# The up-projection of a convolutional FFN: seven quarter products in place of eight, gated activations kept in DRAM

## The chip, the cores and the metric

One core of a Trainium2 chip. The program is launched once and runs from start to end without loops at run time. The metric is the device time of one run in microseconds (us); before, three runs were taken, and their median counts.

## The reference, cut to what matters

Float32, 1024 tokens of 1024 features. Two layers (gated spatial mixing and attention side by side), one layer of gated linear attention (GLA), then the FFN that the change is about, then a last norm:

```python
def conv_ffn(x, w_up, conv_w, conv_b, w_down):
    s = x.shape[1]
    u = x @ w_up                                   # [1024, 1024] @ [1024, 5632]
    u_pad = jnp.pad(u, ((0, 0), (CONV_WIDTH - 1, 0), (0, 0)))
    u = sum(u_pad[:, j:j + s] * conv_w[j] for j in range(CONV_WIDTH)) + conv_b
    gate, up = jnp.split(u, 2, axis=-1)            # 2816 columns each
    return (jax.nn.silu(gate) * up) @ w_down       # [1024, 2816] @ [2816, 1024]
```

The input of `conv_ffn` is `rms_norm(x, norm2)`, and its output is added to `x`.

## The kernel before, in words

**Products.** A float32 product runs as three matmuls over an exact split `x = hi + lo` (`hi` is `x` rounded to float32r): hi·hi, hi·lo and lo·hi (`steps3`, L158). `split` (L71) makes the pair from a float32 tile: a cast for `hi`, on VectorE (DVE) at L75 or on ScalarE (ACT) at L73, and a subtraction for `lo` on DVE through `tt` (L57). Every matmul is issued at L63, in `mm`. TensorE is PE, its weight loads PEld; GpSimd is POOL.

**Order.** PE's instructions run in the order in which they are written (a manual schedule). For the other engines and for the DMA queues (nearly all transfers are issued by SyncE, SP) a scheduler sets the order at build time, from its own simulated times, the written order being the priority; each engine then runs its list strictly in that order, and waits are semaphores on tiles. Tiles come from pools by tag, each tag with a number of buffers (`bufs`); a new tile of a tag waits until the last readers of the buffer's former tile are done.

**Activations.** The normed activations are held transposed, features on the partitions: two slots `X0` and `X1` of 32 KiB per partition (`big`, L105), one for each half of the tokens, each with hi and lo, 8 feature tiles and 512 tokens. In other stages the same slots hold the attention's probabilities (`XB`, L438, and `XA`, L562), in the FFN's second half the split gated tiles and the sums (`gX`, L937, `acc`, L946). `to_T` (L142) transposes four tiles of 128x128 on PE into PSUM and splits them into the slot.

**Weights.** `Weights` (L112) streams packed chunks of 128x1024 float32 (512 KB) through buffers `raw` (2) and splits them into pairs `w` (3).

**Start.** 20 float32 products of the identity with itself (`N_WARM`, L249) keep PE busy while the first token tile and its weights arrive.

**Output projection of the GLA** (L863 to L883): eight token tiles; beside each, on PE, the transposes of a former tile's normed result (`turn_x`, L854), which fill `hT`, the FFN's input. The last tile's norm is made in tile `gpost` (L884) and is transposed within the FFN (L929). At the end of the last tile, `W.fill(3)` (L882) fetches the first three chunks of `w_up`.

**Up-projection** (L924 to L940). `w_up` is packed so that chunk 2i is a block of 128 gate columns and chunk 2i + 1 the block of 128 up columns that belongs to it, each with all 8 feature tiles; 44 chunks, 22 pairs. For each chunk and each half of the tokens `up_mm` (L903) issues 24 matmuls of 128x512 into a PSUM tile `u` of 128x1024. The first three chunks run over the first half of the tokens, then the transposes of the last token tile, then over the second half. `up_use` (L906) works on a finished `u`: ACT starts the convolution (`c = u * cw2 + cb`), DVE adds two shifted products (L911, L912); after the up block of a pair ACT makes a tanh and DVE two gate steps, the last into `gs` (L917), a tile that keeps all 22 gated blocks in SBUF (88 KB per partition).

**Down-projection** (L969 to L1000). For each half of the output columns, for each two of the 22 gated blocks: a chunk of `w_down` is split, `gsplit` (L919) splits two blocks of `gs` into two of four slots (cast and subtraction on DVE), and PE issues 48 matmuls into eight PSUM banks, one for each token tile. At the end the sums, the residual `acc` and the last norm.

Of the kernel before, what the change touches and what calls it, by code (L numbers as in the profile page):

```python
# [8 lines left out]
F32 = mybir.dt.float32  # L9
# [9 lines left out]
NT = 8  # L19
KT = 8  # L20
FT = 22
N_WARM = 20
# [14 lines left out]
def build(tc, a):  # L37
    """The whole forward pass on one core.

    Float32 products run as three float32r passes over an exact split x = hi + lo  # L40
    (hi = x rounded to float32r, lo = x - hi): hi*hi + hi*lo + lo*hi.
    """
# [62 lines left out]
    def big(i, dt=F32R):  # L105
        """One of the two 32 KiB slots that hold h^T, the attention's P^T and P, the last gate and sums."""
        return T(xpool, [128, 8192], f"X{i}", dt)

    def hT_half(i):
        return big(i).rearrange("p (s k t) -> p s k t", s=2, k=KT)  # L110
# [31 lines left out]
    def to_T(src, dst, c0, ps_pool, n, k0=0, tag="tr"):  # L142
        """dst[:, hi/lo, k0 + k, c0:c0 + 128] = src[:, 128 k:128 (k + 1)]^T, k < n."""
# [7 lines left out]
    def norm_scale(xt, xn, g, junk=None):  # L151
        """xn = rmsnorm(xt) * g"""
# [27 lines left out]
    class Norms:  # L180
        """The token tiles of one norm, two ahead of their transposes into h^T."""
# [19 lines left out]
        def turn(self, j, tag="tr"):  # L201
# [3 lines left out]
            to_T(self.ready[t][:, 512 * j:], self.hT[t // 4], (t % 4) * 128, self.ps, 4, 4 * j, tag)  # L205
# [11 lines left out]
    # ------------------------------------------------------------------ the first two layers  # L217
# [3 lines left out]
    W = Weights(["w_in0", "w_out0", "w_in1", "w_out1", "gla_w_in", "gla_w_out", "w_up", "w_down"],  # L221
# [4 lines left out]
    for l in range(2):  # L226
# [11 lines left out]
        # A: norm, projections, gated spatial mixing  # L238
# [6 lines left out]
        if l == 0:  # L245
# [100 lines left out]
        def rope(dst, sq, qn, ps, n, i, t):  # L346
            """dst = rope(rmsnorm(ps) * g) of n heads of 64 for token tile t; sq and qn are for its use."""
# [27 lines left out]
        def turn_k(t):  # L375
            """K^T of the two heads, each in both halves of the partitions."""
# [34 lines left out]
        def gate_b(u, ps, th):  # L411
            """silu(g_b)^T * 2, a block of 128 features by 512 tokens; 4 steps."""
            hf, j = 1 - u // 4, u % 4
            for k in range(0, KT, 2):
                steps3(ps, wcols(ws[j:j + 1], 128), lambda k, s: hT[hf][:, s, k, :], range(k, k + 2), 0, KT - 1)
# [15 lines left out]
        # B: attention and, one token tile behind, the output projection  # L431
# [6 lines left out]
        XB = big(1, F32).rearrange("p (u k) -> p u k", u=8)  # L438
        qf, ya = XB[:, 7, 0:512], XB[:, 7, 512:1024]
# [13 lines left out]
        def scores(g):  # L453
            """Group g = (token tile, kv head): S, its maximum, exp; 8 steps."""
# [3 lines left out]
            for hh in (0, 2, 1, 3):  # L458
# [9 lines left out]
                P[hh] = XB[:, count[1] % 7]  # L468
# [10 lines left out]
        def turn(g, u):  # L479
            """P^T of two heads for two key tiles, split; the gate over the row sums first."""  # L480
# [10 lines left out]
            PT = XA[:, count[0] % 8]  # L491
# [41 lines left out]
        def project(qt):  # L533
            """x_new(t) = x(t) + rmsnorm(y(t) w_out) * g_post; 16 steps."""
# [27 lines left out]
        XA = big(0).rearrange("p (u s k h t) -> p u s k h t", u=8, s=2, k=2, h=2)  # L562
# [4 lines left out]
        def step(*ks):  # L567
            """The next step of the oldest projection, if it is one of these, once for each unit (g, u)."""
# [7 lines left out]
        for g in range(2 * NT):  # L576
# [6 lines left out]
            for u in range(8):  # L583
# [33 lines left out]
    # ------------------------------------------------------------------ gated linear attention  # L617
# [27 lines left out]
    def f3(ps, L, R, start=True, stop=True):  # L645
        """ps (+)= L^T R of hi/lo pairs."""
# [65 lines left out]
    def chunks(h, v, rs, kT, sT, qq, gd):  # L712
        """The chunks of head h and their gated norm; two steps each."""
# [30 lines left out]
    for h in range(4):  # L744
# [4 lines left out]
        def of(x):  # L749
            """The hi and lo parts of tile t of a pair."""  # L750
# [20 lines left out]
        # k and q: feature-major, with their decays  # L771
# [313 lines left out]
```

## Time and profile before

| | |
|---|---|
| runs | 2269.79 us median of 3 (2268.68 to 2269.9) |
| profiled execution, first to last instruction (span) | 2268.4 us |
| the median of the runs over the profiled span | 1.4 us |
| up-projection in that execution | 1541.2 to 2020.9 us |
| down-projection and end | 2020.9 to 2268.4 us |

The profiled execution is known by its span alone: the clock of a run also takes in what lies around the first and the last instruction. In the rows below times are us from the span's start, unless marked ns; "x" is a number of instructions; `<-` in a name reads "written from", and after a bracket or bar it names what ended the wait. A matmul's own duration (389 ns) is longer than its share of a full queue, since matmuls overlap.

### The profile page before, as it was taken

The page shows a single profiled execution, that of the slowest core. Times are in us where ns is not written, and L with a number is a line of the kernel's source. Part 1 is how long each engine was busy: PE and PEld are TensorE (multiplying, and loading weights), DVE is VectorE, ACT ScalarE, POOL GpSimd, SP SyncE. Part 2 cuts the span into 40 slices and gives each one's busy share as a digit, 9 for nine tenths or more (in the row PEclk, how much of TensorE's full clock was granted, in tenths as well). Part 3 has the DMA queues.
Part 4 walks back from the last instruction along what each step waited for, and adds up shares of the span by engine and source line. Part 5 has one row for each costly group of instructions (what it writes and reads, how often), then busy time and mean ns, then how long its engine had stood idle before and what let it go on. Part 6 is the DMA issues. An engine that isn't in the chain of part 4 may idle for free.

```text
span 2268.4 us, 30078 instructions
## 1 busy us (share of the span) xinstructions
PE 2239.4 (99%) x12196; PEld 1923.9 (85%) x12196; DVE 1420.0 (63%) x2169; ACT 747.8 (33%) x1401; POOL 157.3 (7%) x210
## 2 busy tenths in 40 slices
PE   9999999999999999999999999999999999999998
PEld 7888888888788878888899999888888888888887
DVE  7545788888844578888755655645554555554644
ACT  4203276665212146666532322221111111111102
POOL 1004200000101500000100100100000000000000
PEclk9999999999999999999999999999999999999999
DMA  5131401114321231111411112532111111131111
GB/s 191 62 122 38 158 24 58 56 37 145 114 72 65 75 126 43 43 56 63 154 45 59 47 56 78 175 102 76 54 49 47 47 47 56 47 121 47 47 56 75
DMA packets 65036, 171.93 MB, mean 76 GB/s; under 512 B 7680, under 2 KB 20352, under 8 KB 64896
## 3 DMA queue, kind: packets, MB, share of 16 engines
q1 hardware_dynamic: 63888, 166.33, 22.0%
q10 hardware_dynamic: 1008, 3.67, 0.6%
q8 instruction: 96, 1.57, 0.3%
q14 instruction: 44, 0.36, 0.1%
HBM read 136.94 MB, written 33.03 MB: 75 GB/s over the span
## 4 chain that ended last, share of the span: by engine, by line
PE 92%; DVE 3%; ACT 2%; issue 1%; DMA 1%; POOL 0%; POOLq 0%; SPq 0%; ACTq 0%; DVEq 0%
PE mm L63 33%; PE u L63 21%; PE d L63 10%; PE po L63 7%; PE o L63 7%; PE S L63 6%; PE tr L490 4%; PE tr L147 1%; DVE X L57 1%; ACT X L66 1%; DVE nm L467 0%; POOL rs L57 0%; PE big L63 0%; ACT X L73 0%; PE tr L405 0%
## 5 line engine op out<-in xcount | busy, mean ns | idle before, releaser
L63 PE MATMUL mm<-w,X 128*128 128x512 f32 (+1 forms) x3072 | 552.2, 338 | 2.3 <-DVE w L57 1.3
L63 PEld LDWEIGHTS mm<-w,X 128*128 128x128 f32 x3072 | 476.7, 190 | 64.0 <-DVE w L57 2.1
L63 PE MATMUL u<-X,w 128*128 128x512 f32 x2112 | 479.3, 389 | 0.8 <-DVE xt L57 0.8
L63 PEld LDWEIGHTS u<-X,w 128*128 128x128 f32 x2112 | 396.2, 188 | 83.4 <-DVE xt L57 1.2
L57 POOL TENSOR_TENSOR rs<-ve,nhalf 128x1 f32<-128x1 f32 (+2 forms) x136 | 109.8, 808 | 2078.6 <-DVE ve L93 2077.7
L63 PE MATMUL d<-w,X 128*128 128x512 f32 x1056 | 240.0, 389 | 0.2 <-DVE X L57 0.2
L57 DVE TENSOR_TENSOR X<-tr,X 128x512 fp32r<-128x512 f32 x300 | 204.4, 684 | 47.9 <-ACT X L73 44.9
L63 PEld LDWEIGHTS d<-w,X 128*128 128x128 f32 x1056 | 198.0, 188 | 41.9 <-DVE X L57 0.9
L75 DVE CAST w<-raw 128x1024 fp32r<-128x1024 f32 x132 | 93.2, 707 | 214.6 <-PE u L63 192.7
L73 ACT CAST X<-tr 128x512 fp32r<-128x512 f32 x300 | 173.5, 585 | 142.1 <-PE tr L490 77.4
L57 DVE TENSOR_TENSOR w<-raw,w 128x1024 fp32r<-128x1024 f32 x160 | 195.3, 1222 | 3.5 <-ACT w L73 1.0
L63 PE MATMUL S<-K,qT 128*128 128x512 f32 x512 | 178.9, 430 | 2.6 <-DVE t L60 1.4
L467 DVE TENSOR_REDUCE nm<-S 128x1 f32<-128x1024 f32 x128 | 155.9, 1218 | 25.6 <-PE S L63 25.2
L63 PEld LDWEIGHTS po<-X,V 128*128 128x128 f32 x1024 | 151.6, 189 | 22.8 <-DVE ol L57 6.8
L63 PE MATMUL po<-X,V 128*128 128x256 f32 x1024 | 167.7, 287 | 2.0 <-DVE ol L57 1.8
L66 ACT ACTIVATE X<-S,nm 128x1024 f32<-128x1024 f32 x128 | 142.9, 1116 | 62.2 <-DVE nm L467 62.0
L66 ACT ACTIVATE c<-u,cb,cw 128x1024 f32<-128x1024 f32 x44 | 53.2, 1208 | 317.5 <-PE u L63 317.5
L63 PE MATMUL mm<-X,w 128*128 128x512 f32 x672 | 155.5, 390 | 0.0
L490 PE MATMUL tr<-ident,X 128*128 128x128 f32 x960 | 144.7, 273 | 4.7 <-ACT qT L406 2.1
L63 PEld LDWEIGHTS mm<-X,w 128*128 128x128 f32 x672 | 125.3, 188 | 25.5
L490 PEld LDWEIGHTS tr<-ident,X 128*128 128x128 f32 x960 | 110.7, 139 | 12.4 <-DVE X L57 3.9
L60 DVE SCALAR_TENSOR_TENSOR c<-u,cw,c 128x1023 f32<-128x1023 f32 x88 | 112.6, 1280 | 1.5
(207 smaller groups left out, 2302.2 us busy)
## 6 DMA issues: line engine op xcount, KB each, us to landing
raw<-w_in SPq DMA_DIRECT2D x46, 512.0 KB, 3.5
raw<-w_up SPq DMA_DIRECT2D x44, 512.0 KB, 3.3
xt<-x SPq DMA_DIRECT2D x37, 512.0 KB, 3.7
raw<-gla_w_in SPq DMA_DIRECT2D x24, 512.0 KB, 3.6
raw<-w_down SPq DMA_DIRECT2D x22, 512.0 KB, 3.3
raw<-w_out SPq DMA_DIRECT2D x16, 512.0 KB, 3.3
x<-xt SPq DMA_DIRECT2D x16, 512.0 KB, 2.6
y<-yA SPq DMA_DIRECT2D x16, 256.0 KB, 2.0
```

What stands on the lines that cost most here:

```text
L57: (eng or nc.vector).tensor_tensor(out=out, in0=in0, in1=in1, op=op)
L60: nc.vector.scalar_tensor_tensor(out=out, in0=in0, scalar=scalar, in1=in1, op0=op0, op1=op1)
L63: nc.tensor.matmul(out, lhsT, rhs, start=start, stop=stop)
L66: nc.scalar.activation(out=out, in_=in_, func=func, **kw)
L73: nc.scalar.copy(hi, src)
L75: nc.vector.tensor_copy(hi, src)
L147: nc.tensor.transpose(ps[:, k], src[:, (j + k) * 128:(j + k + 1) * 128], ident)
L467: nc.vector.reduce_max(out=nm, in_=ps, axis=AX.X, negate=True)
L490: nc.tensor.transpose(ptr[:, k, e], P[pr + 2 * e][:, kt * 128:kt * 128 + 128], ident)
```

## The change

`w_up` and the activations are each taken as a 2x2 matrix of quarters: activations A11, A12 (first 512 tokens; first and last 512 features), A21, A22 (last 512 tokens), weights of a pair B11, B21 (up columns; first and last 512 features) and B12, B22 (gate columns). Eight products of quarters become seven, in Winograd's form of Strassen's algorithm: S1 = A21 + A22, S2 = S1 - A11, S3 = A11 - A21, S4 = A12 - S2; T1 = B12 - B11, T2 = B22 - T1, T3 = B22 - B12, T4 = B21 - T2; P1 = A11·B11, P2 = A12·B21, P3 = S4·B22, P4 = A22·T4, P5 = S1·T1, P6 = S2·T2, P7 = S3·T3. The results are up, first half: P1 + P2; gate, first half: P1 + P6 + P5 + P3; gate, second half: P1 + P6 + P7 + P5; up, second half: P1 + P6 + P7 + P4. P1, P6, P7 and P4 add up in one PSUM bank, which is read between them; P5 and P3 in another.

With it: the slots `X0`, `X1` become four quarter slots, here and in all earlier stages; S1 and S3 of the last four token tiles are formed while these are transposed; the sums of weights are made by POOL; `gs` goes to DRAM block by block, and `gsplit` loads it back and casts on ACT; `acc` gets a tile of its own; 10 warm-up products in place of 20, and seven wide ones.

The diff (comments, docstrings and what only follows the new slots are left out):

```diff
-N_WARM = 20
+N_WARM = 10
...
-    def big(i, dt=F32R):
-        return T(xpool, [128, 8192], f"X{i}", dt)
+    def quarter(i, dt=F32R):
+        return T(xpool, [128, 4096], f"X{i}", dt)
+    def hT_quarter(i):
+        return quarter(i).rearrange("p (s k t) -> p s k t", s=2, k=4)
     def hT_half(i):
+        return [hT_quarter(2 * i), hT_quarter(2 * i + 1)]
...
+            wide = [T(psL, [128, 512], "mm", bufs=6) for _ in range(2)]
+            for _ in range(3):
+                mm(wide[0], identr, identr.unsqueeze(1).broadcast_to([128, 4, 128]), True, True)
+            for _ in range(2):
+                for e in range(2):
+                    r = identr[64 * e:64 * e + 64]
+                    mm(wide[e], r, r.unsqueeze(1).broadcast_to([64, 4, 128]), True, True)
...
-    hT = [hT_half(0), hT_half(1)]
+    A11, A12, A22 = (hT_quarter(i) for i in range(3))
+    sums = quarter(3, F32).rearrange("p (s k t) -> p s k t", s=2, k=4)
+    S1f, S3f = sums[:, 0], sums[:, 1]
...
+    def quarters(t, xn, ps_pool):
+        if t < 4:
+            for j, A in enumerate((A11, A12)):
+                to_T(xn[:, 512 * j:], A, t * 128, ps_pool, 4)
+                yield
+            return
+        c = slice((t - 4) * 128, (t - 3) * 128)
+        p21 = four_T(xn, ps_pool)
+        tt(S3f[:, :, c], A11[:, 0, :, c], p21, ALU.subtract)
+        nc.scalar.copy(S1f[:, :, c], p21)
+        tt(S3f[:, :, c], S3f[:, :, c], A11[:, 1, :, c], ALU.add)
+        yield
+        p22 = four_T(xn[:, 512:], ps_pool)
+        split(A22[:, 0, :, c], A22[:, 1, :, c], p22, on_act=True)
+        tt(S1f[:, :, c], S1f[:, :, c], p22, ALU.add)
+        yield
...
+    def up_load(p):
+        raws[p] = [T(pF, [128, 1024], "rawx", bufs=2) if p % 2 else T(W.p, [128, 1024], "raw", bufs=2)
+                   for _ in range(2)]
+        for i in range(2):
+            load(raws[p][i], a["w_up"][2 * p + 1 - i])
+    def w_pair(i):
+        if i in (3, 5) or i > 5 and i % 4 == 1:
+            return T(pU, [128, 2, 1024], "wx", F32R)
+        return T(W.p, [128, 2, 1024], "w", F32R, bufs=3)
...
-                W.fill(3)
+                up_load(0)
+                ops[0] = [w_pair(0)]
+                split(ops[0][0][:, 0], ops[0][0][:, 1], raws[0][0], on_act=True)
...
-    gs = T(pF, [128, FT, 1024], "gs")
+    g_d = T(dram, [FT * 128, 1024], "gs")
...
+    def up_ops(p):
+        r1, r2 = raws.pop(p)
+        lo, hi = slice(0, 512), slice(512, 1024)
+        w = ops.setdefault(p, [])
+        if not w:
+            w.append(w_pair(3 * p))
+            split(w[0][:, 0], w[0][:, 1], r1, on_act=True)
+        t23 = T(pU, [128, 1024], "t23")
+        tt(t23[:, hi], r2[:, hi], r2[:, lo], ALU.subtract, nc.gpsimd)
+        tt(r2[:, lo], r2[:, lo], r1[:, lo], ALU.subtract, nc.gpsimd)
+        tt(t23[:, lo], r2[:, hi], r2[:, lo], ALU.subtract, nc.gpsimd)
+        tt(r1[:, hi], r1[:, hi], t23[:, lo], ALU.subtract, nc.gpsimd)
+        for src in (r2, t23):
+            w.append(w_pair(3 * p + len(w)))
+            split(w[-1][:, 0], w[-1][:, 1], src, on_act=True)
+        w.append(T(pU, [128, 2, 512], "w4", F32R, bufs=2))
+        split(w[3][:, 0], w[3][:, 1], r1[:, hi], on_act=True)
+    def product(ps, p, i, half, A, first, last=True):
+        w = ops[p][i]
+        c = 512 * half
+        for k in range(4):
+            L = [w[:, s, c + 128 * k:c + 128 * k + 128] for s in range(2)]
+            R = [A[:, s, k, :] for s in range(2)]
+            for n, (x, y) in enumerate(((0, 0), (0, 1), (1, 0))):
+                nc.tensor.matmul(ps, L[x], R[y], start=first and k == n == 0, stop=k == 3 and n == 2,
+                                 skip_group_check=True)
+    def bank(tag):
+        return T(psU, [128, 512], tag, bufs=3)
+    def P1(p):
+        s = st[p] = {"a": bank("a"), "up": T(pU, [128, 1024], "up", bufs=2)}
+        product(s["a"], p, 0, 0, A11, True)
+        nc.scalar.copy(s["up"][:, t1], s["a"])
+    def P2(p):
+        b = bank("b")
+        product(b, p, 0, 1, A12, True)
+        add(st[p]["up"][:, t1], b)
+    def P5(p):
+        s = st[p]
+        s["c"], s["gate"] = bank("b"), T(pU, [128, 1024], "gate", bufs=2)
+        product(s["c"], p, 1, 0, S1, True)
+        nc.scalar.copy(s["gate"][:, t2], s["c"])
+    def P6(p):
+        s = st[p]
+        product(s["a"], p, 2, 0, S2, False)
+        nc.scalar.copy(s["gate"][:, t1], s["a"])
+    def P3(p):
+        s = st[p]
+        product(s["c"], p, 1, 1, S4, False)
+        add(s["gate"][:, t1], s.pop("c"))
+    def P7(p):
+        s = st[p]
+        product(s["a"], p, 2, 1, S3, False)
+        add(s["gate"][:, t2], s["a"])
+    def P4(p):
+        s = st[p]
+        product(s["a"], p, 3, 0, A22, False)
+        nc.scalar.copy(s["up"][:, t2], s["a"])
     def gsplit(n):
-        gT = gX[:, n % 4]
-        split(gT[:, 0], gT[:, 1], gs[:, n % FT])
+        raw = T(pF, [128, 1024], "rawx", bufs=2)
+        load(raw, tok(g_d, n % FT))
+        gT = gX[n % 4]
+        split(gT[:, 0], gT[:, 1], raw, on_act=True)
         return gT
+    def conv(u, j, tag):
+        c = T(cst, [128, 1024], tag)
+        act(c, u, AF.Identity, scale=cw[:, j, 2:3], bias=cb[:, j:j + 1])
+        stt(c[:, 1:], u[:, :1023], cw[:, j, 1:2], c[:, 1:], ALU.mult, ALU.add)
+        stt(c[:, 2:], u[:, :1022], cw[:, j, 0:1], c[:, 2:], ALU.mult, ALU.add)
+        return c
+    def gated(p):
+        g = conv(st[p].pop("gate"), p, "gpre")
+        th = st[p]["th"] = T(pU, [128, 1024], "th")
+        act(th, g, AF.Tanh, scale=0.5)
+        stt(th, th, 1.0, g, ALU.add, ALU.mult)
+    def stored(p):
+        s = st.pop(p)
+        c = conv(s["up"], FT + p, "gpost")
+        stt(s["th"], s["th"], 0.5, c, ALU.mult, ALU.mult)
+        load(tok(g_d, p), s["th"])
+        del ops[p]
+    up_ops(0)
+    up_load(1)
+    P1(0)
+    P2(0)
+    up_ops(1)
+    for _ in quarters(NT - 1, xn, psU):
+        pass
+    P1(1)
+    P2(1)
+    for p in range(2):
+        b = bank("b")
+        product(b, p, 3, 0, A22, True)
+        nc.scalar.copy(st[p]["up"][:, t2], b)
...
+    for k in pairs:
+        split_sum(S1, k, S1f[:, k])
+    for s2, k in zip(tmp, pairs):
+        tt(s2, S1f[:, k], A11[:, 0, k], ALU.subtract)
+        tt(s2, s2, A11[:, 1, k], ALU.subtract)
+        split_sum(S2, k, s2)
+    for k in pairs:
+        split_sum(S3, k, S3f[:, k])
+    S4 = hT_quarter(3)
+    for s2, k in zip(tmp, pairs):
+        tt(s2, A12[:, 0, k], s2, ALU.subtract)
+        tt(s2, s2, A12[:, 1, k], ALU.add)
+        split_sum(S4, k, s2)
...
+    P5(0)
+    P5(1)
+    P6(0)
+    P7(0)
+    sum21(0)
+    P3(0)
+    gated(0)
+    stored(0)
+    up_load(2)
+    P6(1)
+    P7(1)
+    sum21(1)
+    up_ops(2)
+    P3(1)
+    gated(1)
+    stored(1)
+    for p in range(2, FT):
+        if p + 1 < FT:
+            up_load(p + 1)
+        P1(p)
+        P2(p)
+        P5(p)
+        if p > 2:
+            P4(p - 1)
+            stored(p - 1)
+        P6(p)
+        if p + 1 < FT:
+            up_ops(p + 1)
+        else:
+            W.fill(2, True)
+        P3(p)
+        P7(p)
+        gated(p)
...
+    gTs = [gsplit(k) for k in range(2)]
+    P4(FT - 1)
+    stored(FT - 1)
     sU.close()
...
-    acc = big(1, F32).rearrange("p (t c) -> p t c", t=NT)
+    acc = T(pD, [128, NT, 1024], "acc")
```

(`xn` is the normed tile; `split_sum` splits two of four feature tiles of a sum on ACT and DVE; `sum21` adds bank `a` to `up`'s second half; `pairs` are the two halves of the feature tiles, `tmp` two tiles of 128x1024.)

## Rows read from the trace of the kernel before

**Rows 1.** The page: span, and each engine's busy time, share and instructions.

```profile
span 2268.4 us, 30078 instructions
PE 2239.4 (99%) x12196; PEld 1923.9 (85%) x12196; DVE 1420.0 (63%) x2169; ACT 747.8 (33%) x1401; POOL 157.3 (7%) x210
```

**Rows 2.** Chain that ended last, 1500 to 2060 us: start, duration, what.

```profile
1541.19 11.19 PE u L63 x48
1552.37 0.87 PE tr L147 x8
1553.25 467.85 PE u L63 x2064
```

**Rows 3.** Windows: stretch, length, busy PE, PEld, DVE, ACT, POOL, clock, DMA share, GB/s.

```profile
1541.20:2020.90 479.70, 479.70 (x2120) 397.32 (x2121) 247.90 (x224) 77.40 (x69) 0.55 (x1) 1.00 0.15 50
```

**Rows 4.** Waits of PE, 1541 to 2030 us: in total, times, longest.

```profile
PE u L63 <- DVE xt L57: 0.8, 1, 0.8
```

**Rows 5.** Groups by shape, 1541 to 2021 us: busy us, mean ns, idle before.

```profile
L60 DVE SCALAR_TENSOR_TENSOR c<-u,cw,c 128x1022 f32<-128x1022 f32 x43 | 55.1, 1281 | 1.5
...
L57 DVE TENSOR_TENSOR w<-raw,w 128x1024 fp32r<-128x1024 f32 x43 | 52.7, 1226 | 1.4
L66 ACT ACTIVATE c<-u,cb,cw 128x1024 f32<-128x1024 f32 x43 | 52.0, 1208 | 312.2 <-PE u L63 312.2
L75 DVE CAST w<-raw 128x1024 fp32r<-128x1024 f32 x43 | 29.8, 694 | 192.7 <-PE u L63 192.7
L60 DVE SCALAR_TENSOR_TENSOR th<-th,c 128x1024 f32<-128x1024 f32 x22 | 27.0, 1225 | 23.7 <-ACT th L66 23.7
...
L66 ACT ACTIVATE th<-c 128x1024 f32<-128x1024 f32 x22 | 23.3, 1061 | 74.6 <-DVE c L60 74.6
```

**Rows 6.** Groups by shape, whole span: operations that the change issues more of.

```profile
L57 DVE TENSOR_TENSOR X<-tr,X 128x512 fp32r<-128x512 f32 x300 | 204.4, 684 | 47.9 <-ACT X L73 44.9
L73 ACT CAST X<-tr 128x512 fp32r<-128x512 f32 x300 | 173.5, 585 | 142.1 <-PE tr L490 77.4 <-PE tr L147 61.1
L73 ACT CAST w<-raw 128x1024 fp32r<-128x1024 f32 x28 | 29.5, 1053 | 178.7 <-PE d L63 174.2 <-DMA raw<-w_in 3.7 <-PE S L63 0.6
L57 DVE TENSOR_TENSOR xt<-xt,mm 128x512 f32<-128x512 f32 x16 | 11.0, 688 | 21.2 <-PE mm L63 19.9 <-DMA xt<-x 1.2
```

**Rows 7.** Line 57 on POOL: duration ns min/median/max, first and last start, shape.

```profile
L57 POOL TENSOR_TENSOR sq<-qn,tab x32: 730/1180/1582, 196.8 to 793.2; 128x256 f32<-128x256 f32 x32
...
L57 POOL TENSOR_TENSOR t<-t,tab x12: 313/325/375, 166.0 to 733.8; 128x64 f32<-128x64 f32 x12
```

**Rows 8.** Timeline of DVE and POOL, 196 to 204 and 231 to 247 us.

```profile
196.67 0.69 DVE L57 TENSOR_TENSOR t<-qn,tab 128x512 f32<-128x512 f32 x1
196.78 1.88 POOL L57 TENSOR_TENSOR sq<-qn,tab 128x256 f32<-128x256 f32 x2 [0.87 <-DVE qn L57]
...
234.28 2.73 POOL L57 TENSOR_TENSOR sq<-qn,tab 128x256 f32<-128x256 f32 x2 [0.87 <-DVE qn L57]
235.19 1.23 DVE L57 TENSOR_TENSOR t<-qn,tab 128x512 f32<-128x512 f32 x1
```

**Rows 9.** Timeline at the beginning of the up-projection: the last tile's norm.

```profile
1543.23 1.28 DVE L60 SCALAR_TENSOR_TENSOR gpost<-xt,rs,gpre 128x1024 f32<-128x1024 f32 x1 [0.73 <-POOL rs L57]
```

**Rows 10.** DMA issues: queue, how many, KB each, median us to landing.

```profile
raw<-w_up SPq DMA_DIRECT2D x44, 512.0 KB, 3.3
...
x<-xt SPq DMA_DIRECT2D x16, 512.0 KB, 2.6
```

**Rows 11.** Timeline of the start: warm-up, first norm, first weight cast, first transposes.

```profile
2.68 7.47 PE L63 MATMUL tr<-ident 128*128 128x128 f32 x40 [2.68 <-DMA ident<-cst]
...
7.04 1.28 DVE L60 SCALAR_TENSOR_TENSOR xn<-xt,rs,gpre 128x1024 f32<-128x1024 f32 x1 [0.67 <-POOL rs L57]
8.30 1.05 ACT L73 CAST w<-raw 128x1024 fp32r<-128x1024 f32 x1 [2.11 <-DMA raw<-w_in]
...
9.98 1.04 PE L147 MATMUL tr<-ident,xn 128*128 128x128 f32 x8
```

**Rows 12.** Windows at the start (columns as in rows 3).

```profile
6.00:9.00 3.00, 3.00 (x19) 3.00 (x18) 1.44 (x2) 0.89 (x3) 0.55 (x1) 1.00 1.02 411
```

More of the change, by code (lines that the diff above doesn't have):

```diff
@@ L414, in gate_b @@
             for k in range(0, KT, 2):
-                steps3(ps, wcols(ws[j:j + 1], 128), lambda k, s: hT[hf][:, s, k, :], range(k, k + 2), 0, KT - 1)
+                steps3(ps, wcols(ws[j:j + 1], 128), feat(hT[hf]), range(k, k + 2), 0, KT - 1)
                 if k < KT - 2:
@@ L437, in build @@
         g_pre = bcast(cst, a["pre_g"][1:2, :] if l == 0 else a["norm1"], 1024, "gpre")
-        XB = big(1, F32).rearrange("p (u k) -> p u k", u=8)
-        qf, ya = XB[:, 7, 0:512], XB[:, 7, 512:1024]
+        XB = [x[:, j] for x in (quarter(i, F32).rearrange("p (u k) -> p u k", u=4) for i in (2, 3)) for j in range(4)]
+        qf, ya = XB[7][:, 0:512], XB[7][:, 512:1024]
         count = [0, 0]
@@ L561, in build @@
             next(units[i // 4])
-        XA = big(0).rearrange("p (u s k h t) -> p u s k h t", u=8, s=2, k=2, h=2)
+        XA = [x[:, j] for x in (quarter(i).rearrange("p (u s k h t) -> p u s k h t", u=4, s=2, k=2, h=2)
+                                for i in (0, 1)) for j in range(4)]
         prep_load(0)
@@ L600, in build @@
                     i = NU.index(u) + 1
-                    norms.fetch(XB[:, i])
-                    norms.start(XB[:, i], XB[:, 3 if i < 3 else 4])
+                    norms.fetch(XB[i])
+                    norms.start(XB[i], XB[3 if i < 3 else 4])
         queue.append([project(NT - 1), 0])
@@ L677, in alpha_low @@
                 for s in range(2):
-                    mm(ps, was[:, k], hT[hf][:, s, k, :], k == 0 and s == 0, k == KT - 1 and s == 1)
+                    mm(ps, was[:, k], feat(hT[hf])(k, s), k == 0 and s == 0, k == KT - 1 and s == 1)
             sl = aT[:, hf * 512:hf * 512 + 512]
@@ L857, in turn_x @@
         norm_scale(xts.pop(t), xn, g_pre)
-        for j in (0, 4):
-            to_T(xn[:, 128 * j:], hT[t // 4], (t % 4) * 128, psH, 4, j)
-            yield
+        yield from quarters(t, xn, psH)
+    raws = {}
+    def up_load(p):
[7 more added lines that the diff above has]
+        return T(W.p, [128, 2, 1024], "w", F32R, bufs=3)
+    ops = {}
     xts, yrs = {}, {}
@@ L900, in build @@
     psU = opened_psum(sU, "psU")
[L901 to L917 removed]
+    S1, S2, S3 = (T(pU, [128, 2, 4, 512], f"S{i}", F32R) for i in range(1, 4))
@@ new lines, in product @@
+    def product(ps, p, i, half, A, first, last=True):
+        w = ops[p][i]
+        c = 512 * half
+        for k in range(4):
+            L = [w[:, s, c + 128 * k:c + 128 * k + 128] for s in range(2)]
[5 more added lines that the diff above has]
+        return T(psU, [128, 512], tag, bufs=3)
@@ new lines, in build, with add @@
+    st = {}
+    t1, t2 = slice(0, 512), slice(512, 1024)
+    def add(x, ps):
+        tt(x, x, ps, ALU.add)
+    def P1(p):
[11 more added lines that the diff above has]
+        nc.scalar.copy(s["gate"][:, t2], s["c"])
@@ L919, in gsplit @@
     def gsplit(n):
-        gT = gX[:, n % 4]
-        split(gT[:, 0], gT[:, 1], gs[:, n % FT])
-        return gT
-    first = [(wcols(W.get(1, 2), 128), T(psU, [128, 1024], "u", bufs=3)) for _ in range(3)]
-    for hf in range(2):
-        for n, (w, ps) in enumerate(first):
-            up_mm(ps, w, hf)
-            if hf == 0 and n == 1:
-                to_T(xn, hT[1], 384, psU, KT)
-            if hf == 1:
-                up_use(n, ps)
-    for n in range(3, 2 * FT):
-        w = wcols(W.get(1, 2), 128)
-        ps = T(psU, [128, 1024], "u", bufs=3)
-        up_mm(ps, w, 0)
-        if n == 2 * FT - 1:
-            gX = big(0).rearrange("p (u s k) -> p u s k", u=4, s=2)
-            gTs = [gsplit(k) for k in range(2)]
-        up_mm(ps, w, 1)
-        up_use(n, ps)
+        raw = T(pF, [128, 1024], "rawx", bufs=2)
@@ new lines, in stored @@
+    def stored(p):
[17 more added lines that the diff above has]
+        nc.scalar.copy(st[p]["up"][:, t2], b)
+    pairs = [slice(0, 2), slice(2, 4)]
@@ new lines, in split_sum @@
+    def split_sum(S, k, f):
+        split(S[:, 0, k], S[:, 1, k], f, on_act=True)
+    for k in pairs:
+        split_sum(S1, k, S1f[:, k])
+    tmp = [x.rearrange("p (k t) -> p k t", k=2) for x in (T(cst, [128, 1024], "gpre"), T(pU, [128, 1024], "th"))]
+    for s2, k in zip(tmp, pairs):
[5 more added lines that the diff above has]
+    S4 = hT_quarter(3)
@@ L941, in build @@
+    gX = [x[:, u] for x in (quarter(i).rearrange("p (u s k) -> p u s k", u=2, s=2) for i in (0, 1))
+          for u in range(2)]
+    gTs = [gsplit(k) for k in range(2)]
+    P4(FT - 1)
+    stored(FT - 1)
     sU.close()
```

38 lines of the change are left out of this document (15 added, 23 removed).

## Prediction

> **What bounds the kernel now.** I read the page's busy shares first. TensorE (PE) is busy 2239.4 of a span of 2268.4 us; the next engine, VectorE (DVE), is at 63% [rows 1]. Then the chain of waits, cut to the stage that the change rewrites: from 1541.19 to 2021.10 us the chain is nothing but the up-projection's own matmuls, 48 of them, eight transposes, then 2064 in one piece of 467.85 us [rows 2]. That piece gives the price used below: 467.85 / 2064 = 0.2267 us per matmul of 512 columns in a full queue. The rows by window say what else is busy there: DVE 247.9, ScalarE (ACT) 77.4 and GpSimd (POOL) 0.55 of 479.7 us, at a granted clock of 1.00 [rows 3]. The waits of PE in the stage come to one, 0.8 us [rows 4]. So the stage is PE's, DVE is half idle in it, and a matmul taken out is worth its full price until another engine comes last.
>
> **PE.** Per pair (a block of 128 gate columns and one of 128 up columns) before: 2 blocks x 2 halves x 24 = 96 matmuls, 21.76 us. After: seven products of 12, so 84, 19.04 us. Over 22 pairs 264 matmuls go: 264 x 0.2267 = **-59.8 us**. Their form (128 columns of weights, 512 moving) stays.
>
> The Trainium skill, "TensorE: Matmul & The Clock Gate", section "Wait — 56ns, not 53.3ns?", gives 215.7 ns between the starts of such warm matmuls; by that figure the term would be an estimate of -56.9 us. The trace has 0.2267 us for the same thing, so the trace is used.
>
> **DVE in the steady part.** Before, per pair: two casts 0.69, two subtractions 1.23, four convolution steps 1.28, two gate steps 1.23, together 11.4 us [rows 5]. After: the casts go to ACT; three subtractions of 1024 columns (3.69) and one of 512 (0.68), three additions from PSUM of 512 columns (3 x 0.69), the same four convolution steps (5.12) and two gate steps (2.46): 14.0 us [rows 5, 6]. **ACT**: four copies of 512 from PSUM (2.36), casts 3 x 1.05 + 0.59, two convolution starts 2.42, a tanh 1.06: 9.6 us. Both lie beside 19.04 us of PE.
>
> **POOL**, idle in this stage before, gets four subtractions of 128x512 per pair. No row has this shape. With 256 columns the shortest took 0.730 us and with 64 columns 0.313 [rows 7]; the line through both gives an estimate of 1.29 us for 512, so 5.2 us per pair. But POOL and DVE get in each other's way: at 196.78 two 256-column POOL operations took 1.88 us beside a DVE operation of 0.69; at 234.28, where DVE was working without a pause, two took 2.73, and DVE's `t<-qn,tab` took 1.23 in place of 0.69 [rows 8]. So DVE loses about 0.54 us to a POOL operation of 0.73, all but 0.19 of it. For 1.29 us that makes 1.1, and 4.4 per pair if DVE never has a pause: 14.0 + 4.4 = 18.4, still under 19.04. Since DVE has pauses, I price the steady part by the waits of the stage before, which were none behind the first: 0.1 us per pair, **+2 us** over 20 pairs. Ends: 0, and 1.1 per pair (22 us).
>
> What is queued behind the new waits: ACT's casts of the POOL results stand in ACT's order among the four PSUM copies that PE needs. The tightest is P6's copy, which must leave the bank before P7 writes it; only P3 lies between, 2.72 us. The others have two products or more (5.4 us): P1's copy before P6, P5's before P3, the addition after P7 before the next pair's P4 (three products). The weights have two to five products between their buffer's release and their use.
>
> **The beginning of the stage.** S1 to S4, sums of quarters of the activations, exist only when the last token tile is normed, and DVE makes most of them. PE has work without them: P1 and P2 of two pairs, the eight transposes, P4 of two pairs; then P5, P5 (needs S1), P6 (S2), P7 (S3), P3 (S4). It reaches P3 of pair 0 after ten products and 0.87 us of transposes: 28.1 us after 1541.2. The last tile's norm is done at 1544.5 [rows 9], before PE asks for it at 1546.6, as P1 and P2 of pair 0 cover it. DVE's work to S4: norm 1.4, splits of pair 1 4.4, two additions 1.4, the tile's quarters 4 x 0.69 = 2.8, S1 two subtractions 2.5, S2 four steps and two splits 7.4, S3 2.5, S4 7.4: 29.6 us. Of the first 5.4 us it can use some 2.7, so S4 is there after 32.4: 4.3 us late. To this come POOL's eight or so subtractions in the same stretch; half of one pair's 4.4 us is 2.2. **+6.5 us**, between 1.5 (no pause) and 13 (two pairs' POOL work in full). POOL's and SP's queues are passed here too: POOL's chain for pair 0 may stand ahead of the last norm's power; the 2.1 us between 1544.5 and 1546.6 cover one subtraction, the rest is in the upper end.
>
> **Down-projection.** The gated tiles come from DRAM, 44 loads on SP's queue, cast by ACT (1.05) in place of DVE (0.69). A step of two tiles is 48 matmuls, 10.9 us; three loads of 512 KB land in 3.3 us each [rows 10], 9.9 even one after the other, ACT needs 3.2, DVE 3.7. Each pair's store (2.6 us) goes out some 5.6 us after its P4, in the same pair, so the weight loads behind it on SP's queue are still a pair ahead of need. Cost 0, hidden by a whole step; were that cover gone, a load, cast and subtraction, 5.6 us, once at the stage's start. The last pair's tile is read 100 us after it is stored.
>
> **The start and the slots.** Ten of the 20 warm-up products go (40 matmul records took 7.47 us [rows 11], so 3.7 off), seven of 512 columns come (1.6 at 0.2267). The first transposes could begin up to 1.5 us sooner, as `xn` is there at 8.3 and they start at 9.98. But the first product waits for weights whose cast starts with the DMA's landing, and the DMA engines are full in that stretch [rows 12]. I take 0, ends -1.5 and +0.5. The quarter slots in place of half slots let buffers go at the same readers; the extra DVE steps of tiles 4 to 6 (1.4 us each) fall into DVE's pauses of the output projection: 0, ends -1 and +2.
>
> **Sum** against the profiled span: 2268.4 - 59.8 + 2 + 6.5 = 2217.1 us. The median of the runs, 2269.79, lies 1.4 above that span: **2218.5 us**. This case by itself spans 2209 to 2228.
>
> **Rivals.** *DVE and POOL become the bound* (0.20). For: rows 8, and nearly every DVE operation of the pair reads two tiles in SBUF (11.9 of 14.0 us). If POOL's whole 5.2 us stands against DVE, the pair takes 19.2, and with some 0.9 us for hand-overs among POOL, ACT and DVE 20.1 in place of 19.04: 20 x 1.1 = 22 us in place of 2, so about **2238**. Against: DVE pauses at each pair, and POOL's chain can run a pair ahead.
> The Trainium skill, "SBUF — State Buffer", section "Who interferes with whom", has this as a rule: a DVE instruction with two SBUF inputs and a GpSimd instruction that reads SBUF shut each other out for a whole instruction. By that rule the trace agrees: 0.69 became 1.23.
>
> *No stall at the beginning* (0.06): the scheduler puts the S sums ahead of pair 1's splits, P3 waits 1.5 us, and the start gains 1: about **2211**.
>
> *ACT's queue holds PE* (0.04, slower). If each POOL subtraction first waits for a DVE operation of 1.23, the chain takes 4 x 2.52 = 10.1 in place of 5.2, 4.9 late; a cast waiting for it at the head of ACT's queue keeps P6's copy, and P7 stands 4.9 + 0.6 - 2.7 = 2.8 us in each of 20 pairs. With the beginning at its upper end: 2268.4 - 59.8 + 56 + 13 + 1.4 = **2279**. It decides from a lateness of about 2.1 us on. Against: the buffers let the chain run a pair ahead. In part (0.02) it would end within 0.2% of before.
>
> That the products don't fall away is excluded: the new loops issue 84 matmuls per pair.
>
> **The numbers.** Forecast 0.68, DVE and POOL 0.20, no stall 0.06, ACT 0.04, even 0.02. A measurement of this kernel can tell about 0.2% (4.5 us) from no change. Faster 0.94, same 0.02, slower 0.04. The range 2208 to 2240 holds all of the first and third case and somewhat over half of the second.
>
> **What would show it.** 1848 matmuls over `a` and `b` banks with some 0.227 us each; PE's idle time in the stage in one place, before P3 of pair 0 and perhaps P6; from pair 2 on a period of 19.0 to 19.2 us; POOL at about 1.3 us, longer where DVE is full; DVE at 75 to 95%. A period of 20 us or more with DVE over 95% is the first rival; PE waiting for ACT's copy before P7 in each pair is the last. The forecast is wrong if the down-projection waits for the reloaded tiles, which I price at nothing.

## The result, and the profile after

Before 2269.23 us (2266.42 to 2269.9), after **2240.39 us** (median of four runs, 2235.01 to 2241.39); ratio 0.9873, 95% interval 0.9859 to 0.9887. The change gains 28.8 us where 51.3 were forecast, and 2240.39 lies 0.39 above the top of the range.

The page of the kernel after, span and busy shares (before: [rows 1]):

```profile
span 2237.8 us, 30206 instructions
...
PE 2196.8 (98%) x11919; PEld 1877.1 (84%) x11919; DVE 1525.4 (68%) x2215; ACT 924.3 (41%) x1631; POOL 315.2 (14%) x298
```

The stage by windows, columns as in [rows 3]: the whole up-projection, its beginning (first P1 to P1 of pair 2), a steady part:

```profile
1541.10:1990.80 449.70, 437.52 (x1858) 351.33 (x1857) 382.25 (x313) 214.32 (x257) 160.26 (x89) 0.98 0.25 86
1541.10:1599.90 58.80, 48.05 (x178) 35.84 (x176) 49.11 (x44) 27.45 (x34) 21.38 (x13) 0.88 0.16 54
1631.00:1943.00 312.00, 312.00 (x1350) 253.17 (x1349) 263.24 (x211) 148.43 (x180) 115.55 (x64) 1.00 0.24 83
```

The stage takes 449.7 us where 479.7 stood [rows 3]. In the steady part PE has no gap at all: 312.00 busy of 312.00. In the beginning it has, and its granted clock is 0.88 on average: about 14 of the 58.8 us ran at the lower of the two levels, which is half the upper one. The 14 products and eight transposes there would take 14 x 12 x 0.2267 + 0.87 = 39.0 us in a full queue; they took 58.8, **19.8 too long**; the forecast had +6.5.

The waits of PE in the stage (us in total, times, longest), where [rows 4] had one of 0.8:

```profile
PE b L988 <- DVE S L57: 2.1, 1, 2.1
PE a L988 <- ACT gate L1021: 2.1, 2, 1.3
PE b L988 <- ACT w L73: 2.1, 1, 2.1
PE a L988 <- DVE S L57: 1.8, 1, 1.8
PE b L988 <- DVE X L57: 1.2, 1, 1.2
PE a L988 <- DVE gate L57: 0.9, 1, 0.9
PE a L988 <- ACT S L73: 0.6, 1, 0.6
PE a L988 <- DVE wx L57: 0.6, 1, 0.6
PE b L988 <- ACT gate L1016: 0.5, 1, 0.5
PE b L988 <- ACT S L73: 0.2, 1, 0.2
```

All but two lie in the beginning; 0.9 (DVE's `gate`) stands before the last P4, 0.5 (L1016) before P3 of pair 2. Those of the beginning add up to 10.7 us. They stand in P1 of pair 1 (`wx`), at P4 of both pairs (`X`, `w`), in P5 and P6 of pair 0 (`S`) and before P7 of both (L1021, the copy of P6's result). P3 of pair 0, where the forecast had the wait, starts at 1587.20 and waits for nothing. The other 9 of the 19.8 us go with the lower clock and dearer matmuls; no run parts the two.

Now the chain in the steady part (start, duration, what), against [rows 2]:

```profile
1634.21 5.54 PE a L988 x24
1639.76 5.49 PE b L988 x24
1645.25 5.60 PE a L988 x24
1653.65 5.53 PE a L988 x24
...
1990.93 216.73 PE d L63 x956
```

24 matmuls take 5.49 to 5.60 us, 0.229 to 0.233 each; 0.2267 would make 5.44. This pair takes 1653.65 - 1634.21 = 19.44 in place of 19.04 (19.45 on average), and PE waits for nothing. Over 20 pairs that is **8 us** which the forecast did not have. The down-projection begins at 1990.8 and runs 247.0 us to the end; before, 247.5 [rows 3, with the span of rows 1].

Why the beginning is long shows in its timeline (start, duration, engine):

```profile
1543.53 0.55 POOL L57 TENSOR_TENSOR rs<-ve,nhalf 128x1 f32<-128x1 f32 x1 [11.69 <-DVE ve L93]
1544.05 1.28 POOL L57 TENSOR_TENSOR t<-raw 128x512 f32<-128x512 f32 x1
1544.11 2.30 DVE L60 SCALAR_TENSOR_TENSOR gpost<-xt,rs,gpre 128x1024 f32<-128x1024 f32 x1 [0.73 <-POOL rs L57]
1545.41 2.14 POOL L57 TENSOR_TENSOR raw<-raw,raw 128x512 f32<-128x512 f32 x1
1546.34 2.30 DVE L57 TENSOR_TENSOR wx<-rawx,wx 128x1024 fp32r<-128x1024 f32 x1
1547.63 2.15 POOL L57 TENSOR_TENSOR t<-raw 128x512 f32<-128x512 f32 x1
1548.67 2.20 DVE L57 TENSOR_TENSOR w<-raw,w 128x1024 fp32r<-128x1024 f32 x1
...
1553.23 1.60 POOL L57 TENSOR_TENSOR t<-rawx 128x512 f32<-128x512 f32 x1 [1.23 <-DVE w L57]
...
1557.64 2.12 POOL L57 TENSOR_TENSOR rawx<-rawx,t 128x512 f32<-128x512 f32 x1
1559.79 0.62 ACT L73 CAST w<-rawx 128x512 fp32r<-128x512 f32 x1 [2.53 <-POOL rawx L57]
1560.46 4.62 PE L988 MATMUL b<-X,w 128*128 128x512 f32 x12 [2.09 <-ACT w L73]
```

DVE operations of 1.23 to 1.28 us [rows 5, 9] take 2.20 to 2.30 beside POOL, POOL's 1.28 becomes 2.15: they take turns. POOL's chain for pair 0 starts only behind the last norm's power (1543.53); that for pair 1 waits until DVE has read `t` (1553.23), ends near 1559.8, and P4 of pair 1 stands 2.09 us for it, then runs 4.62 us for 12 matmuls, since the clock has fallen (P2 of pair 0, at the upper level, took 2.88). An operation of DVE with two inputs in SBUF loses 0.9 to 1.1 us here beside POOL's, and POOL's loses as much beside DVE's. The rule cited with the first rival (the Trainium skill, "SBUF — State Buffer", section "Who interferes with whom") has a DVE instruction with two SBUF inputs and a GpSimd instruction that reads SBUF shut each other out; these rows agree.

### The profile page after: what moved, and what is told of

Read it like the earlier page. It is cut to its first block, busy times and chain, and to the rows that moved or that the text cites. A ratio compares the mean times of both kernels' runs of the same rounds, so it can differ in the third digit from the quotient of the medians.

```text
span 2237.8 us, 30206 instructions
## 1 busy us (share of the span) xinstructions
PE 2196.8 (98%) x11919; PEld 1877.1 (84%) x11919; DVE 1525.4 (68%) x2215; ACT 924.3 (41%) x1631; POOL 315.2 (14%) x298
## 5 line engine op out<-in xcount | busy, mean ns | idle before, releaser
L57 DVE TENSOR_TENSOR w<-raw,w 128x1024 fp32r<-128x1024 f32 (+1 forms) x144 | 180.1, 1252 | 21.2 <-ACT w L73 20.1
L57 DVE TENSOR_TENSOR X<-rawx,X 128x1024 fp32r<-128x1024 f32 x44 | 53.6, 1221 | 126.6 <-ACT X L73 126.5
L988 PE MATMUL b<-X,w 128*128 128x512 f32 x420 | 104.2, 397 | 3.9 <-ACT w L73 2.1
L988 PE MATMUL a<-X,w 128*128 128x512 f32 x432 | 105.9, 394 | 0.9 <-DVE gate L57 0.9
L66 ACT ACTIVATE t<-mm 128x512 f32<-128x512 f32 (+1 forms) x34 | 18.4, 542 | 210.7 <-PE mm L63 168.7
L73 ACT CAST X<-rawx 128x1024 fp32r<-128x1024 f32 x44 | 45.9, 1048 | 140.7 <-PE d L63 137.7
```

The source lines that it names most:

```text
L57: (eng or nc.vector).tensor_tensor(out=out, in0=in0, in1=in1, op=op)
L66: nc.scalar.activation(out=out, in_=in_, func=func, **kw)
L73: nc.scalar.copy(hi, src)
L988: nc.tensor.matmul(ps, L[x], R[y], start=first and k == n == 0, stop=k == 3 and n == 2, skip_group_check=True)
```

## The experiments

Ratios are to the kernel before, run beside each. "Pair" is the steady period, "beginning" as above; both are read from the starts of the products in the traces. "Stage" is the time from the first P1 to the first matmul of the down-projection, 449.6 after the change. For effects of a few us it tells more than the time of a run: in the kernels made from the changed one the first P1 begins anywhere from 1537.1 to 1543.2, with the same instructions before it. Addresses are those that the build gave the tiles. In the changed kernel X0 to X3 and `w` start 96 bytes past a multiple of 256, S1 to S3, `wx` and `w4` at a multiple of 256; in the kernel before, slots and `w` both 96 past one.

**1. Place.** The padding moves S1 to S3, `wx` and `w4` by 160 bytes; no instruction changes.

```diff
-    cb = T(pF, [128, 2 * FT], "cb")
+    cb = T(pF, [128, 2 * FT + 40], "cb")[:, 0:2 * FT]
```

> One tile of small constants gets 160 bytes more per partition, so that S1 to S3, `wx` and `w4` move by 160 bytes and lie like the X quarters and `w` (same rest by 256, 512 and 1024 bytes); no instruction changes. In the changed kernel a steady pair takes 19.45 us where 84 x 0.2267 = 19.04 was forecast, and the matmuls that read S, `wx` or `w4` stand 0.231 to 0.238 us apart, those that read X and `w` 0.2267. Theory (place): a matmul whose moving tile and weights lie at different rests is slower. Then a steady pair takes 19.0 to 19.1 us and the whole 20 x 0.4 = 8 us less, about 2232. Rival (hand-over): the time goes at the waits between products, of which there are now seven per pair and were four. Then the pair stays at 19.45 and the whole at 2240.

2230.69 us, ratio 0.9837 [0.9823, 0.9852]; pair 19.04, beginning 58.1, stage 443.7. The chain of this kernel, one pair of the steady part and the start of the next:

```profile
1649.34 5.44 PE a L988 x24
1654.78 5.44 PE b L988 x24
1660.22 5.44 PE a L988 x24
1668.38 5.44 PE a L988 x24
```

Every 24 matmuls take 5.44: the old price is back, and with it the 8 us of the pairs. The waits at the beginning stay. The stage is shorter by 6.0 us only, since the last P4 now waits 1.8 us and runs at the lower clock behind that (4.4 us to the next product); the rest of what the profiled run gains lies before the stage.

**2. The same with 32 bytes.**

```diff
-    cb = T(pF, [128, 2 * FT], "cb")
+    cb = T(pF, [128, 2 * FT + 8], "cb")[:, 0:2 * FT]
```

> The same edit as the run with 160 bytes of padding, with 32 bytes: S1 to S3, `wx` and `w4` move to addresses that leave 224 by 256 and 96 by 128; the quarters and `w` leave 96 by both. If what counts is that the two operands of a matmul leave the same by 256, the products stay at 0.230 to 0.235 us and the pair near 19.4 us, the time at that of the changed kernel (2238 to 2242). Rival: if it counts by 128 only, every product goes to 0.227, the pair to 19.04, and the time to some 2231, as with 160 bytes.

2235.3 us, 0.9853 [0.9839, 0.9866]; pair 19.37, stage 448.1; products of a moved and an unmoved operand at 0.229 to 0.238 in turn, products of S with `wx` (both moved) at 0.227. The rest by 128 does not decide it. The time is some 3 us under the expected one, though the stage is 1.6 us shorter only: its first product begins at 1537.1, 4 us sooner than after the change, a difference of the stages before.

**3. The kernel before, moved.**

```diff
     pW = opened(top, "pW")
+    T(pW, [128, 40], "pad")
```

> The kernel before, with 160 bytes of padding ahead of its weight buffers and not one instruction changed: `w` then leaves 0 by 256, X0 and X1 leave 96 as before. If the place of the two operands sets the price of a matmul, the old up-projection (2112 matmuls of `w` with the slots) goes from 0.2267 to 0.231 to 0.234 us each, 9 to 16 us more in that stage, as much again per matmul in the down-projection (1056) and in the projections of the layers before (some 2200): 20 to 40 us in all, 2290 to 2308. Rival: the dearer matmuls come from the change's own tiles and their mixed order, not from the place: then this kernel stays at 2267 within 0.2%.

2303.99 us, ratio 1.0156 [1.0143, 1.017]: 35 us slower with the same instructions, as expected. Its chain, beside [rows 2]:

```profile
1552.84 11.46 PE u L63 x48
1565.17 481.60 PE u L63 x2064
```

481.60 / 2064 = 0.2333 in place of 0.2267. The place sets the price, in the old kernel too.

**4. The price by itself.** 48 matmuls for each of 64 places, with nothing else at work; `A` and `W` are the placed tiles, `run` issues 48 matmuls, in the order of four products.

```diff
+    for w in W:
+        for x in A:
+            run(x, w)
+            n += 1
```

> The price of a matmul by place, by itself: nothing of the forward pass is computed. Eight moving tiles (mA to mH, each hi and lo, four blocks of 512 columns) and eight tiles of weights (wA to wH) begin at addresses that leave 0, 96, 160, 224, 256, 352, 416 and 480 by 512; each of the 64 combinations runs 48 matmuls in the order of a product of the kernel, with nothing else at work. If equal rests by 512 make the fast price, the eight of like letters take 48 x 0.2267 = 10.9 us each, and the others 11.1 to 11.3 (0.231 to 0.236). If it is by 256, also 0 with 256 (A with E), 96 with 352 (B with F), 160 with 416 (C with G) and 224 with 480 (D with H) are fast. Rival: a tile has to stand at certain rests by itself, whatever the other's; then whole letters are fast or slow.

Groups by shape (busy us, mean ns of one), weights `wA` at rest 0, moving tiles `mA`, `mB`, `mC`, `mE` at 0, 96, 160, 256:

```profile
L106 PE MATMUL b<-mC,wA 128*128 128x512 f32 x48 | 11.4, 396 | 0.0
L106 PE MATMUL b<-mB,wA 128*128 128x512 f32 x48 | 11.4, 395 | 0.0
...
L106 PE MATMUL b<-mA,wA 128*128 128x512 f32 x48 | 11.1, 390 | 0.0
...
L106 PE MATMUL b<-mE,wA 128*128 128x512 f32 x48 | 11.1, 389 | 0.0
```

(Busy time holds the last matmul's tail.) Mean ns between starts, by rest of the address by 512:

```
weights \ moving    0     96    160    224    256    352    416    480
    0             227.5  233.6  234.2  233.4  227.2  233.6  234.2  233.4
   96             234.3  227.0  229.2  232.5  234.2  227.0  229.2  232.5
  160             233.6  233.3  227.1  229.2  233.5  233.3  227.1  229.2
  224             233.0  233.3  233.1  227.6  233.4  232.2  233.6  227.6
```

(Weights at 256 to 480 repeat these rows within 0.3.) Where the rests by 256 are equal, a matmul costs 227.0 to 227.6 ns, else 229 to 234; no tile is fast or slow by itself. The Trainium skill, "SBUF — State Buffer", section "Who interferes with whom", gives TensorE two independent read ports, one for the moving operand and one for loading weights. In these rows the price hangs on the two addresses together, and the measurement decides. By what mechanism it does is not shown.

**5. The sums of weights on DVE.**

```diff
-        tt(t23[:, hi], r2[:, hi], r2[:, lo], ALU.subtract, nc.gpsimd)
+        tt(t23[:, hi], r2[:, hi], r2[:, lo], ALU.subtract)
...
```

> The four subtractions of each pair's weights run on DVE in place of POOL. In the changed kernel the beginning of the stage (first P1 to P1 of pair 2) takes 58.7 us where 14 products and 8 transposes are 39.0. Theory (shared way): it is late because POOL and DVE shut each other out there (DVE subtractions of 2.2 to 2.3 us in place of 1.2, POOL's of 2.15 in place of 1.28) and the weights of pairs 0 and 1 hang on POOL's chain. Then DVE takes 8 x 0.69 = 5.5 us more of its own and loses no 1.0 us six to eight times; with POOL's latency gone the beginning gets 5 to 9 us shorter; the steady pairs stay (DVE 16.8 of 19.4): about 2233. Rival (DVE's own work): the sums S1 to S4 alone set the end; then the beginning gets 3 to 5 us longer: about 2244.

2230.86 us, 0.9838 [0.9823, 0.9853]; beginning 52.1 (-6.7), stage 442.6, pair unchanged at 19.45. The steady part by window, as above:

```profile
1631.00:1943.00 312.00, 312.00 (x1350) 253.22 (x1349) 253.63 (x274) 148.98 (x177) 0.00 (x0) 1.00 0.24 81
```

DVE issues 63 instructions more and is busy *less* than after the change, 253.6 in place of 263.2: POOL's help cost it more than the work itself (an estimate: 64 x 0.69 = 44 us). At the beginning the longest wait is now 3.8 us for the split of A22, which stands on DVE behind pair 1's sums.

**6. No sums for pairs 0 to 2.**

```diff
-        t23 = T(pU, [128, 1024], "t23")
...
+        t23 = r1 if p < 3 else T(pU, [128, 1024], "t23")
+        if p >= 3:
+            tt(t23[:, hi], r2[:, hi], r2[:, lo], ALU.subtract, nc.gpsimd)
...
```

> For pairs 0 to 2 the sums of weights are left out (the products take the weights as they come, so part of the computation is missing); the rest as in the changed kernel. Theory (shared way): the beginning loses all of POOL's chain, 8 us or more shorter: 2232 or less. Rival (DVE's own work): S1 to S4 stay, and the beginning gets 2 us shorter at most: 2238 or more. Against the kernel with the sums on DVE it shows what DVE's 5.5 us of sums cost: by the first theory 2 to 5 us.

2225.62 us, 0.9816 [0.98, 0.9833]; beginning 46.6 (-12.2), stage 437.0, clock at its upper level throughout. This kernel leaves out part of the computation and only serves to price it. So of the 19.8 us too many, 12.2 come from the sums and what their waits did to the clock, 6.7 of these from their being on POOL; 7.6 remain, with waits of 3.0 for the copy of P6's result, 1.4 for `X`, 0.8 for `S` and 0.3 for `wx`, and under 1 us of the dearer products.

**7. The clock.** 41 spare matmuls of 512 columns on PE where it waits.

```diff
+    def fill(ps, n):
+        for _ in range(n):
+            nc.tensor.matmul(ps, identr, A11[:, 0, 0, :], start=True, stop=True, skip_group_check=True)
...
```

> 41 matmuls of 512 columns without use are put before P4 of pairs 0 and 1 (5 and 9), before P5 (10), P6 (11) and P7 (6) of pair 0, where PE waited 1.2, 2.1, 2.3, 2.4 and 1.3 us, so that PE does not pause. In the changed kernel the granted clock was at the half level in four stretches of the beginning, 13.7 us in all, after PE's waits, and P7 of pair 0 took 5.5 us in place of 2.7. Theory (clock): without the pauses the clock stays at its full level and the beginning gets 2 to 6 us shorter, about 2236. Rival (DVE sets the end anyway): what the clock gives back is waited for instead, 2240, or a little more where the added matmuls outlast a wait (up to 2 us).

2242.23 us, 0.9886 [0.9872, 0.9901]; beginning 62.1 (+3.3), stage 453.0. The window of the beginning:

```profile
1541.00:1610.00 69.00, 60.52 (x249) 46.17 (x248) 56.92 (x50) 32.28 (x39) 25.46 (x16) 0.98 0.18 62
```

The clock stayed up (0.98), and the kernel was no faster: though the spare matmuls filled 41 x 0.2267 = 9.3 us, PE still waited over 8 us in the beginning, 5.3 of them for the copies in place of 2.1. That a raised clock by itself gives the time back is refuted; what the clock gave was waited for instead. Since the spare matmuls take time themselves, the run does not price the lower clock.

**8. Both remedies** (padding of 160 bytes, sums on DVE).

> Both remedies in one kernel: the 160 bytes of padding and the four sums of weights on DVE. If the two losses are apart (place: the steady pairs; POOL's lock on DVE: the beginning), the gains add: 9.7 for the padding and 9.5 for the sums, 2240.4 - 19.2 = 2221, 2219 to 2224. Rival: both gains come out of the same waits; then it stays at 2228 to 2231.

2220.16 us, 0.9785 [0.9772, 0.9798]: the gains add (20.2 us, 9.7 and 9.5 one by one); pair 19.04, beginning 50.5, stage 432.9.

**9. Last tile ahead of pair 1's sums**, from that kernel.

```diff
-    up_ops(1)
+    ops[1] = [w_pair(3)]
+    split(ops[1][0][:, 0], ops[1][0][:, 1], raws[1][0], on_act=True)
     for _ in quarters(NT - 1, xn, psU):
         pass
+    up_ops(1)
```

> The kernel of the run with both remedies, and the transposes and splits of the last token tile put ahead of the second pair's sums of weights in the written order. There PE waited 3.8 to 4.1 us for the split of A22 (before P4 of pair 0), with the second pair's sums ahead of it on DVE. If DVE's total work in the beginning sets the end, this wait only moves to S1 to S4 and the gain is 0 to 1 us. If the order sets it, 2 to 4 us go: 2217 to 2219.

2218.72 us, 0.978 [0.9767, 0.9793]; beginning 49.3, stage 431.9: 1.4 us less than run 8, between the two expectations and within the noise. The wait for A22 is gone; in its place PE waits 4.6 us for `w` of pair 1's P4.

**10 and 11. PE's order changed**, from run 9's kernel: the products of pairs 0 and 1 in turn. In run 10 (its edit is shown) both P3 stand last, in run 11 P3 of pair 0 stands ahead of P7 of pair 1:

```diff
+    P40(0)
...
+    P5(0)
+    up_ops(1)
+    P40(1)
+    P5(1)
...
     P6(0)
+    P6(1)
...
```

> From the kernel with the order changed: PE's products of pairs 0 and 1 alternate (P4 of 0, P5 of 0, P4 of 1, P5 of 1, P6 of 0, P6 of 1, P7 of 0, P7 of 1, P3 of 0, P3 of 1), and the splits of S1 stand ahead of the second pair's sums. If the work that DVE has in front of S4 sets the end of the beginning, the end is where DVE is done, and PE's order can hide at most the 4.6 us it waited for the second pair's T4 and the 1.4 us for the copies between P6 and P7: the beginning goes from 49.2 to 44 to 46 us, the time to 2214 to 2217. Rival: pair 2's first weights now wait for the buffer that P3 of pair 0 gives back later, and the wait moves there: 2218 to 2222.

> The same with P3 of pair 0 ahead of P7 of pair 1: S4 is wanted one product sooner, pair 2's weight buffer comes free one product sooner. If S4 is what comes last, this is 0 to 3 us slower than the other order; if the weight buffer is, 0 to 3 us faster.

2218.91 us, 0.9783 [0.9769, 0.9796], and 2218.69 us, 0.978 [0.9767, 0.9794]; beginning 49.3 and 49.2, stage 431.6 and 431.5: a miss, nothing gained. Waits and window of run 11:

```profile
PE b L988 <- ACT w L73: 3.1, 1, 3.1
...
PE b L988 <- DVE S L57: 1.5, 1, 1.5
PE b L988 <- DVE w L57: 1.0, 1, 1.0
```

```profile
1541.00:1581.00 40.00, 33.88 (x138) 26.20 (x137) 38.37 (x44) 20.71 (x27) 0.30 (x1) 0.91 0.18 57
```

DVE is busy 38.4 of 40 us. Behind P5 of pair 1 PE waits no more, but it has waited for S1 and for pair 1's sums before. In each of the three orders tried (runs 9 to 11) some operand is late, while DVE is nearly full.

**12. Place in the layers before**, from run 11's kernel.

```diff
                     yb = yTs[qt, 1] = T(pB, [128, 2, 4, 128], "yb", F32R)
+                    T(pB, [128, 32], "pad")
...
     yTs = {0: [T(pY, [128, 2, 4, 128], f"yT{j}", F32R) for j in range(2)]}
+    T(pY, [128, 32], "pad")
```

> From the kernel with P3 of pair 0 ahead of P7 of pair 1: padding of 128 bytes behind the transposed tiles of the layers before (`ya`, `yb`, `yT0`, `yT1`), so that these too leave 96 by 256, as the weights do. Nothing else changes. 384 + 624 + 144 = 1152 matmuls of 512 columns read these tiles, with 0.2314 to 0.2328 us each in place of 0.2267: if the place sets the price, 1152 x 0.0057 = 6.6 us go, 2212 (2210 to 2214), in stages that the change did not touch. Rival: those stages are held by DVE and ACT, so that PE's gain turns into waits there: 2216 to 2219.

2221.28 us, 0.9795 [0.9782, 0.9808]; stage 431.1: a miss, 2.6 us above the kernel it started from. The products `mm<-w,yT` fell from 232.7 to 228.7 ns between starts, and their stage (the GLA's output projection) from 102.3 to 100.9 us; but that stage began 4.0 us later than in run 11, for a reason that is open. The 624 `o<-w,ya` and `o<-w,yb`, 232.7 before, stayed at 232.5 to 233.0 although the rests by 256 are equal now. They are issued three at a time between transposes and products of other tiles, which the padding left or moved elsewhere. Whether that is what keeps them dear is open. That S·`wx` cost 230 ns in the changed kernel, at equal rests (0 and 0), among products of unequal ones, points the same way, and so does `S<-K,qT` in the moved kernel before (its 14 shortest spacings of 256 went from 227 to 233 ns, though the rests are equal: 96 and 96 before, 0 and 0 there), but no run separates it.

## Why the prediction went wrong

- **264 matmuls less, -59.8: right in number, wrong in price for the rest.** The step "Their form (128 columns of weights, 512 moving) stays" took the form for the price. The 1848 matmuls kept the form and changed the place: S1 to S3, `wx` and `w4` are new tiles whose addresses do not agree with their partners'. That made 8 us over the steady pairs; runs 1, 3 and 4 show the cause.
- **The beginning, +6.5: 19.8 measured; the mis-sized term.** "Half of one pair's 4.4 us is 2.2" priced the sums there; run 6 gives 12.2 for them, and run 5 puts 6.7 of these on POOL. The loss of each operation beside POOL's was forecast well (1.1, measured 0.9 to 1.1). The path was wrong: the forecast had PE run until P3 of pair 0 and wait there once, for S4. PE waited at P4 to P7 instead, and came to P3 so late (46.1 us behind the first P1, forecast 28.1) that S4 was there. What the forecast lacked: POOL's chain runs one pair behind the other through the one `t23` buffer, and its lateness reaches PE through `w4`, ahead of S4; DVE's pauses at 1557.30 and 1560.44 (1.81 and 1.80 us, for ACT's casts of that chain's results) come from it too; and a PE that has waited goes on at the lower clock. Its 4.3 for DVE's own work stands against 7.6 without any sums. P6 and P7 follow each other directly there, so that P7 waits for the copy; the forecast looked at that copy with P3 between.
- **The steady part, +2: right in its mechanism.** Two waits, 1.4 us together; DVE at 263.24 / 312 = 84% (75 to 95% forecast), POOL's subtraction 1.28 us alone (1.29 forecast) and 2.15 where DVE is full.
- **DVE and POOL as the bound (2238): its number came out, its mechanism did not.** PE has no gap in the steady part, and with the sums taken off POOL the pair stays at 19.45. The period that was to betray this rival (20 us or more) did not come.
- **ACT's queue holding PE: no.** P7 has no wait from pair 2 on; its waits are the two of the beginning. P3 of pair 2 waits 0.5 us for a copy, once.
- **Down-projection 0: right**, 247.0 against 247.5, with 44 loads more on SP's queue. **Start and slots 0: right**, the first P1 begins at 1541.1 against 1541.19, as far as a start that varies by 6 us among like kernels can tell.

Sum: 2217.1 + 13.3 (beginning) + 8.1 (place) - 0.6 (steady waits) = 2237.9; the span is 2237.8. With both losses mended the kernel runs at 2220.2 (run 8), with the order changed too at 2218.7. That this meets the 2218.5 of the forecast is in part luck: its beginning still has 10 us more than a full queue, the forecast had 6.5. Two small sums of the prediction are off and change nothing: DVE's work to S4 adds up to 29.8 (29.6 there), and the case without a stall to 2212.5 (2211 there).

## What to carry to other kernels

A matmul's price belongs to its shape and to the place of both operands: after any change in allocation, compare the spacing in the steady part with the old one before looking for waits, and try padding that makes the rests by 256 agree (160 bytes did here, 32 did not). Before giving work to POOL, add to it what DVE loses on every operation with two SBUF inputs beside it; here DVE alone was faster than both. A stretch that hides work on average has to be checked at its beginning, where the engines that supply it are nearly full and a chain through a single buffer can set the start.

## What the runs showed of the hardware

- Moving operand and weights at addresses with unequal rests by 256 cost 229 to 234 ns per float32r matmul of 512 columns, where equal ones cost 227 (upper clock level); 160 bytes of padding make a whole kernel 35 us slower (0.2333 against 0.2267 over 2064 matmuls). With products of other places between, equal rests alone did not always suffice; what else is wanted is open.
- DVE with 63 instructions more, and POOL silent, was busy 9.6 us less in 312.
- Behind a wait of 2.1 us PE's granted clock was at its lower level: 12 matmuls took 4.62 us where 12 at the upper level took 2.88. Keeping PE busy through such waits kept the clock up and won no time here.
